# Experts' last sum moved into the matmul accumulator, and the router's last tile taken by halves

## Chip, cores and metric

One core of one Trainium2 chip. The metric is device time of one execution in microseconds (us), the median of several runs. TensorE (PE) multiplies, VectorE (DVE), ScalarE (ACT) and GpSimd (POOL) do the elementwise work, and SyncE (SP) issues the loads from HBM.

## The reference, cut to what matters

256 tokens of width 1024 go through two blocks. In the second layer of the first block a mixer ends in a projection `y @ w_out`, a residual and a layer norm; a router picks two of eight experts for each token; each expert is a gated feed-forward (1024 to 2816 to 1024); the two results are weighed by a softmax over the two logits and summed, and another residual and layer norm follow:

```python
mix = _mixer(u, w_in[layer], ...)                      # ends in  y @ w_out
x = _layernorm(ALPHA * x + (1.0 + g1) * mix, ln1_g, ln1_b)
u = x * (1.0 + sc2) + sh2
top_logits, top_idx = lax.top_k(u @ w_router, 2);  top_w = softmax(top_logits)
ff = sum over the two experts of  top_w * ((silu(u @ Wg) * (u @ Wu)) @ Wd)
x = _layernorm(ALPHA * x + (1.0 + g2) * ff, ln2_g, ln2_b)
```

After that comes a second network, whose first stage is a dense feed-forward on the same `x`.

## The kernel before, in words

Tokens stand in two tiles of 128 (t = 0, 1). Precise products are made of three matmuls (`mm3`, L307): each operand is split into a rounded part "h" and a rest "l", by a ScalarE copy and a VectorE subtraction. For weights these two are L274 and L275, one pair per half unit of 128x1024; they read a raw tile that SP loaded (four raw tiles in turn). Ten half units can be held ahead (`SLOTS`). Every engine works through its own list in the order in which the program wrote it; which half units are converted at which point is written by hand in strings of digits (`TICKS`, one digit per call of `tick`), and `take` forces conversions that have not been made yet.

**The mixer's end** (layer 1). `out_both` L835 projects tile 0 (16 matmuls with 512 columns, L624), takes its residual and statistics (`Norm.stat` L102: L114, L115, bn_stats L123; `fin` L125), and then projects tile 1 with the two halves of the output alternating. After five eighths of tile 1, `Norm1.apply` of tile 0 (L1972) puts its router logits on PE: four transposes L1941, a copy, eight small products L1945, and the same again for the second half; then `settle` L1947. After tile 1 the same follows for tile 1 (`stats` L1957), then `finish` L1981: two scalings L137, the rounding L1987, the residual L1994 and L1995 on VectorE, and only then `settle`. In `moe` (L974) the ranks of both tiles come (L991 to L997, six VectorE operations), the positions (three products L1000 to L1002, a copy L1004), the rest part L1990, the selection matrices `So` (`choose`, four operations L1040), the clearing of the two sums `racc` on GpSimd (L1168), and the gather of the first two experts' tokens (`gather`, 32 matmuls L1070 and L1071), after which the first expert's `gate_up` can start. `load_ahead` (L983) lets SP put later weights into idle tiles, the last two of them into the tiles of the rows G and B that L1994 and L1995 have read.

**The experts' loop** (L1174) runs over 88 chunks, 11 for each expert: `gate_up` of chunk i (24 matmuls), in whose middle the result of chunk i-1 is turned (`turn` L477, hh L315, hl L316), then `down` of chunk i-1 (12 matmuls with 512 columns into two accumulators). Sums of earlier experts are added into `racc` while the next expert runs. In the last expert, chunks 6 and 7 multiply `racc` by the row and add the residual (`residual` L1114). `last` (L1123) then takes the last expert's result: four splits (L315, L316), 16 matmuls with 256 columns through the selection matrix `ST` (L1144, L1145), and per quarter a product with weight and row (L1150), an addition into `racc` (L1152) and bn_stats; after both halves of tile 0 `fin`, the scaling (`scale_all`: L149 and L151, two each) and the turning of x (`to_T`: eight transposes L344, rounding L351, rest L361). Tile 1's norm stands between tile 0's, and its `apply` (scaling and turning) is left in `pend`.

**The feed-forward after it** starts with chunks (tile, chunk) = (0,0), (0,1), (1,0), (1,1); `nxt` in the middle of the first two takes one entry of `pend` each, so that tile 1's `apply` falls into the middle of (0,0).

Of the kernel before, what the change touches and what calls it, by code (L numbers as in the profile page):

```python
# [17 lines left out]
P = 128  # L18
D = 1024
# [47 lines left out]
    "moe_end": "000200000010001",  # L67
# [26 lines left out]
class Norm:  # L94
# [3 lines left out]
    def __init__(self, kern, t, ps, cols, grow=None, mode="T", r=None):  # L98
        self.k, self.t, self.ps, self.cols, self.grow, self.mode = kern, t, ps, cols, grow, mode
        self.r, self.scaled, self.between = r, False, None  # L100
# [18 lines left out]
    def bn(self, hf):  # L119
        k = self.k  # L120
        if hf == 0:
            self.st = k.smp.tile([P, 2, 6], F32, name="st")
        k.nc.vector.bn_stats(out=self.st[:, hf, :], in_=self.r[:, hf * 512:hf * 512 + 512])  # L123
# [16 lines left out]
    def scale_all(self):  # L140
# [7 lines left out]
        for sl in sls:  # L148
            stt(out=r[:, sl], in0=r[:, sl], scalar=self.mv[:, 0:1], in1=k.G[:, sl], op0=ALU.subtract, op1=ALU.mult)  # L149
# [19 lines left out]
class Kern:  # L169
# [317 lines left out]
    def down(self, part, wd, acc, first, last, free, norm=None, mid=None):  # L487

        order = [(i, hf) for hf in range(2) for i in range(2)] if norm else [(i, hf) for i in range(2) for hf in range(2)]
# [126 lines left out]
    def out_proj(self, units, y, acc, kbs, first, last, free, mid=None, ticks=8):  # L616

        for n, kb in enumerate(kbs):
# [17 lines left out]
            if n < ticks:  # L636
                self.tick()

# [11 lines left out]
    def gla_mixer(self, layer, done, start=None, before_out=None):  # L650
# [181 lines left out]
        self.out_both(self.take(4), y, [0, 1, 2, 4, 5, 6, 7, 3], done)  # L832
# [140 lines left out]

    def moe(self, L, gc, bc, grow, done):  # L974

        nc, tc, a, x = self.nc, self.tc, self.a, self.x
        split = self.pend.popleft()
# [8 lines left out]

        gt = self.acp.tile([P, 2, 8, 8], F32, tag="sg", name="gt")
        eq = self.acp.tile([P, 2, 8, 8], F32, tag="sg", name="eq")
        le = L[:, :, :, None].to_broadcast([P, 2, 8, 8])
        lo = L[:, :, None, :].to_broadcast([P, 2, 8, 8])  # L990
        nc.vector.tensor_tensor(out=gt, in0=lo, in1=le, op=ALU.is_gt)  # L991
        nc.vector.tensor_tensor(out=eq, in0=lo, in1=le, op=ALU.is_equal)
        nc.vector.tensor_tensor(out=eq, in0=eq, in1=self.lt[:, None, :, :].to_broadcast([P, 2, 8, 8]), op=ALU.mult)
        nc.vector.tensor_tensor(out=gt, in0=gt, in1=eq, op=ALU.add)
        rank, s1, s2, sel, tmp, W, pos = (sm(n, [P, 2, 8]) for n in ("rank", "s1", "s2", "sel", "tmp", "W", "pos"))
        nc.vector.reduce_sum(out=rank, in_=gt, axis=AX.X)
        nc.vector.tensor_scalar(out=sel, in0=rank, scalar1=2.0, scalar2=None, op0=ALU.is_lt)  # L997
# [3 lines left out]
        nc.tensor.matmul(ps[:, 8:16], self.us, sel[:, 1, :], start=True, stop=False)  # L1001
        nc.tensor.matmul(ps[:, 8:16], self.onesf, sel[:, 0, :], start=False, stop=True)  # L1002
        split()
# [119 lines left out]
        def last(e, acc, norms):  # L1123

            st = ST.pop(e)
            y = []
            for q in range(4):
                if q < 2:
                    yh, yl = (self.acp.tile([P, CW], F32R, tag=g, name="y" + g) for g in ("hh", "hl"))
                else:  # L1130
                    yh, yl = cuts[:, q % 2, 0, :], cuts[:, q % 2, 1, :]
                self.split(yh, yl, acc[q // 2][:, (q % 2) * CW:(q % 2) * CW + CW])
                y.append((yh, yl))
                self.tick(0)
            pss = {}
            for t in range(2):
                ts = slice(t * P, t * P + P)
                for hf in range(2):
                    ps = pss[t, hf] = (self.pgu if t == 0 else self.pacc).tile([P, 512], F32, name="comb",
                                                                               tag="gu" if t == 0 else "acc")  # L1140
                    for q in (0, 1):
                        yh, yl = y[2 * hf + q]
                        pq = ps[:, q * CW:q * CW + CW]
                        nc.tensor.matmul(pq, st[:, ts], yh, start=True, stop=False)  # L1144
                        nc.tensor.matmul(pq, st[:, ts], yl, start=False, stop=True)  # L1145

            def add(t, hf):
                sl = slice(hf * 512, hf * 512 + 512)
                w = mp.tile([P, 512], F32, tag="xs", name="w", bufs=5)
                nc.vector.scalar_tensor_tensor(out=w, in0=pss[t, hf], scalar=W[:, t, e:e + 1], in1=grow()[:, sl],  # L1150
                                               op0=ALU.mult, op1=ALU.mult)
                nc.vector.tensor_tensor(out=racc[t][:, sl], in0=racc[t][:, sl], in1=w, op=ALU.add)  # L1152
                norms[t].bn(hf)
                self.tick(0)
            add(0, 0)
            add(0, 1)
            norms[0].fin()
            self.tick(0)
            norms[0].between = lambda hf: add(1, hf)
            norms[0].apply()  # L1160
            self.tick(0)
            norms[1].fin()
            self.tick(0)
# [5 lines left out]
        for part in range(4):  # L1169
            gather(0, So, part)  # L1170
# [3 lines left out]
        for i in range(n + 1):  # L1174
# [4 lines left out]
            if i < n:  # L1179
# [36 lines left out]
            else:  # L1216
                hT[0] = self.turn(h.pop(i - 1))
            if i:
# [3 lines left out]
                self.down(self.parts_of(hT.pop(0)), self.take(), acc[e], j == 0, j == NCH - 1, True)  # L1222
# [6 lines left out]
        last(NE - 1, acc.pop(NE - 1), norms)  # L1229
        self.close_pool()  # L1230
        self.pend.append(norms[1].apply)
# [629 lines left out]
    def first(self):  # L1861
# [65 lines left out]
        L = self.cp.tile([P, 2, 8], F32, name="L")  # L1927
        mcols = lambda: fold(COL_LN1 + 16, (1, 4), (1, 3))

        class Norm1(Norm):  # L1930
# [16 lines left out]
            def settle(self):  # L1947
                k, t = self.k, self.t
# [7 lines left out]

            def stats(self):  # L1957
                if self.t == 0:
                    return Norm.stats(self)
                for hf in range(2):  # L1960
                    self.stat(hf)
                    self.logits(hf)
                self.fin()
                low, residual = self.finish()
                residual()
                self.settle()
                self.k.pend.append(low)
# [4 lines left out]
            def apply(self):  # L1972
                if self.t == 0:
                    self.logits(0)
                    self.logits(1)
                    self.settle()
                    low, residual = self.finish()
                    residual()
# [211 lines left out]
```

## Time and profile before

| | us |
|---|---|
| median of 3 runs | 2493.15 |
| lowest, highest | 2485.73, 2499.72 |
| the profiled execution's own time | 2487.65 |
| its span (first to last instruction) | 2486.0 |
| PE busy in the span | 2386.9 (96%) |
| DVE, ACT, POOL busy | 1802.7, 1314.6, 44.6 |

The mixer's end lies at about 468 to 507 us of the span, the experts at 507 to 1289, their end and the start of the feed-forward at 1289 to 1328. "Idle before, releaser" in a row says how long the engine had nothing to do before this instruction and what it then waited for.

### The profile page before, as it was taken

To read this page: it belongs to the slowest core of one execution; us is meant where nothing else is said; L and a number is where in the kernel's file an instruction comes from. 1 tells how busy PE (TensorE), PEld (TensorE's weight loads), DVE (VectorE), ACT (ScalarE), POOL (GpSimd) and SP (SyncE) were. 2 spreads that over 40 slices of the span, in tenths; PEclk is the share of its full clock that TensorE was granted. 3 is DMA by queue.
4 is the path that set the end of the run, shared out by engine and by line. 5 is a ranking of instruction groups with operands and counts; after the bars stand their busy time and mean duration, and the time that the engine had idled before them with its cause. 6 is when DMAs were issued, how large, how long until landed. Compare 5 with 4: busy or idle time off the path is not lost. (4 is left out here: it accounts for less than half of the span.)

```text
span 2486.0 us, 34474 instructions
## 1 busy us (share of the span) xinstructions
PE 2386.9 (96%) x13592; PEld 2016.7 (81%) x13592; DVE 1802.7 (73%) x2593; ACT 1314.6 (53%) x1945; POOL 44.6 (2%) x79
## 2 busy tenths in 40 slices
PE   8899989899999999999989999999999998999997
PEld 5769978578788888888867997879987997777996
DVE  6776887689999999999985556555566547556556
ACT  3344444277777777777753444534444444444442
POOL 0000000000000000000000000000000000000000
PEclk9999999899999999999999999999999999999999
DMA  9756957469889999989974544236444644333641
GB/s 361 284 206 241 359 213 277 183 238 371 328 347 372 346 349 364 357 344 358 353 302 169 212 179 167 105 119 246 181 165 160 229 174 149 109 136 124 241 180 62
DMA packets 89208, 600.49 MB, mean 242 GB/s; under 512 B 10288, under 2 KB 11600, under 8 KB 20816
## 3 DMA queue, kind: packets, MB, share of 16 engines
q1 hardware_dynamic: 89040, 598.23, 63.9%
q8 instruction: 108, 1.77, 0.3%
q14 instruction: 60, 0.49, 0.1%
HBM read 597.14 MB, written 1.05 MB: 241 GB/s over the span
## 5 line engine op out<-in xcount | busy, mean ns | idle before, releaser
L275 DVE TENSOR_TENSOR wl<-raw,wh 128x1024 fp32r<-128x1024 f32 (+3 forms) x997 | 1161.4, 1207 | 216.6 <-ACT wh L274 211.0
L274 ACT CAST wh<-raw 128x1024 fp32r<-128x1024 f32 (+3 forms) x997 | 986.6, 1040 | 175.6 <-PE gu L310 99.4
L309 PE MATMUL gu<-uh,wh 128*128 128x256 f32 (+1 forms) x1784 | 504.1, 283 | 0.6 <-ACT cc L785 0.6
L311 PE MATMUL gu<-uh,wl 128*128 128x256 f32 (+1 forms) x1784 | 500.8, 281 | 3.1 <-DVE wl L275 3.1
L310 PE MATMUL gu<-ul,wh 128*128 128x256 f32 (+1 forms) x1784 | 500.3, 280 | 0.0
L309 PEld LDWEIGHTS gu<-uh,wh 128*128 128x128 f32 (+1 forms) x1784 | 334.8, 188 | 6.8 <-issue 1.3
L310 PEld LDWEIGHTS gu<-ul,wh 128*128 128x128 f32 (+1 forms) x1784 | 335.1, 188 | 4.5 <-issue 0.3
L311 PEld LDWEIGHTS gu<-uh,wl 128*128 128x128 f32 (+1 forms) x1784 | 335.5, 188 | 3.8 <-DVE wl L275 3.3
L309 PE MATMUL gu<-wh,xs 128*128 128x512 f32 x704 | 280.8, 399 | 0.1
L311 PE MATMUL gu<-wh,xs 128*128 128x512 f32 x704 | 277.3, 394 | 0.0
L310 PE MATMUL gu<-wl,xs 128*128 128x512 f32 x704 | 276.1, 392 | 0.0
L310 PE MATMUL acc<-wl,hh 128*128 128x512 f32 x432 | 171.2, 396 | 2.6 <-DVE wl L275 2.6
L311 PE MATMUL acc<-wh,hl 128*128 128x512 f32 x432 | 170.5, 395 | 1.6 <-DVE hl L316 1.5
L309 PE MATMUL acc<-wh,hh 128*128 128x512 f32 x432 | 170.9, 396 | 0.5 <-ACT hh L315 0.5
L468 ACT ACTIVATE sg<-gu 128x256 f32<-128x256 f32 x90 | 34.7, 385 | 255.6 <-PE gu L311 255.6
L311 PEld LDWEIGHTS gu<-wh,xs 128*128 128x128 f32 x704 | 132.3, 188 | 29.4
L310 PEld LDWEIGHTS gu<-wl,xs 128*128 128x128 f32 x704 | 132.6, 188 | 26.3
L309 PEld LDWEIGHTS gu<-wh,xs 128*128 128x128 f32 x704 | 132.5, 188 | 26.2 <-issue 0.6
L315 ACT CAST hh<-trh 128x256 fp32r<-128x256 f32 x108 | 40.3, 373 | 198.1 <-PE trh L481 198.1
L311 PE MATMUL acc<-wh,fl 128*128 128x512 f32 x360 | 141.8, 394 | 1.2 <-DVE fl L316 1.2
L309 PE MATMUL acc<-wh,fh 128*128 128x512 f32 x360 | 142.8, 397 | 0.1
L310 PE MATMUL acc<-wl,fh 128*128 128x512 f32 x360 | 141.7, 394 | 0.8 <-DVE wl L275 0.8
(388 smaller groups left out, 3282.4 us busy)
## 6 DMA issues: line engine op xcount, KB each, us to landing
raw<-in_moe_gu_dram SPq DMA_DIRECT2D x175, 1024.0 KB, 5.4
raw<-in_ffn_gu_dram SPq DMA_DIRECT2D x110, 1024.0 KB, 4.9
raw<-in_moe_dn_dram SPq DMA_DIRECT2D x87, 1024.0 KB, 4.9
raw<-in_ffn_dn_dram SPq DMA_DIRECT2D x55, 1024.0 KB, 5.0
raw<-in_ada_w_dram SPq DMA_DIRECT2D x48, 1024.0 KB, 5.2
raw<-in_w_in_dram SPq DMA_DIRECT2D x24, 1024.0 KB, 5.9
raw<-in_fox_in_dram SPq DMA_DIRECT2D x12, 1024.0 KB, 4.9
ww<-in_w_out_dram SPq DMA_DIRECT2D x16, 512.0 KB, 7.4
```

What stands on the lines that cost most here:

```text
L274: nc.scalar.copy(wh[:, :f], r)
L275: nc.vector.tensor_tensor(out=wl[:, :f], in0=r, in1=wh[:, :f].bitcast(F32), op=ALU.subtract)
L309: mm(out, xh, yh, start=first, stop=False)
L310: mm(out, xh, yl, start=False, stop=False)
L311: mm(out, xl, yh, start=False, stop=last)
L315: self.nc.scalar.copy(h, src)
L468: nc.scalar.activation(out=sg, in_=ps[:, :S], func=AF.Silu)
```

## The change

At the mixer's end, tile 1 is projected half by half (`out_halves`), tile 0's logits come after five of the first half's eight matmuls, tile 1's first statistics after the first half and its first logits five matmuls into the second. The ranks are computed per tile in `settle`. The residual of tile 1 is moved behind the gather, as are the clearings of `racc`; the rest part comes before the gather but after `choose`. At the experts' end, `racc` (with the residual) is split into two parts during the last expert and put into the accumulators by products with the identity; the last expert's result is multiplied by weight and row before it goes through `ST`, in halves, behind the first and second half of the last `down`. The norms read the accumulators. Tile 1's scaling is made at once, and its turning moves one chunk later. The digits of `moe_end` put four conversions into the last `gate_up`, and two more are written into the program.

```diff
-    "moe_end": "000200000010001",
+    "moe_end": "220000000000000",
...
     def bn(self, hf):
+        src = self.src[hf] if self.src else self.r[:, hf * 512:hf * 512 + 512]
+        k.nc.vector.bn_stats(out=self.st[:, hf, :], in_=src)
...
     def scale_all(self):
+            stt(out=r[:, sl], in0=self.src[hf] if self.src else r[:, sl], scalar=self.mv[:, 0:1], in1=k.G[:, sl],
+                op0=ALU.subtract, op1=ALU.mult)
...
     def down(...):
+        if norm or then:
+            order = [(i, hf) for hf in range(2) for i in range(2)]
...
+            if then and i == 1:
+                then(hf)
...
+    def out_halves(self, units, y, acc, kbs, mid):
+        for hf in range(2):
+            for n, kb in enumerate(kbs):
...
+                self.nc.tensor.matmul(acc[hf], y(kb), u.halves[half][:, sl], start=n == 0, stop=n == len(kbs) - 1)
+                if hf:
...
+                    if n < 5:
+                        self.tick()
+                if (hf, n) in mid:
+                    mid[hf, n]()
...
     def gla_mixer(...):
-        self.out_both(self.take(4), y, [0, 1, 2, 4, 5, 6, 7, 3], done)
...
+            n0.stats()
+            acc = self.acc2()
+            n1 = done(1, acc)
+            def first_half():
+                n1.stat(0)
+                n0.residual()
+            self.out_halves(uo, y(1), acc, kbs, {(0, 4): n0.apply, (0, 7): first_half,
+                                                 (1, 4): lambda: n1.logits(0)})
+            n1.stat(1)
+            n1.logits(1)
+            n1.fin()
+            n1.settle()
+            n1.scales()
+            self.pend.extend([n1.low, n1.residual])
...
     def moe(...):
+        low, unscaled = self.pend
...
+        nc.tensor.matmul(ps[:, 8:16], self.onesf, sel[:, 0, :], start=True, stop=False)
+        nc.tensor.matmul(ps[:, 8:16], self.us, sel[:, 1, :], start=False, stop=True)
...
+        def base(t):
+            rh = end["h", t] = mp.tile([P, D], F32R, tag="xs", name="rh", bufs=5)
...
+            self.split(rh, rl, racc[t])
+        def slot_weights(e):
+            pc = self.ptr.tile([P, 512], F32, tag="tr", name="cnt")
+            for t in range(2):
+                nc.tensor.matmul(pc[:, 0:1], So[:, t, (e % 2) * P:(e % 2) * P + P].bitcast(F32), W[:, t, e:e + 1],
+                                 start=t == 0, stop=t == 1)
+            ws = end["w"] = sm("ws", [P, 1])
+            nc.vector.tensor_copy(ws, pc[:, 0:1])
...
+        def sums():
+            for t in range(2):
+                for hf in range(2):
...
+                    nc.tensor.matmul(ps, end["i"], end["h", t][:, sl], start=True, stop=False)
+                    nc.tensor.matmul(ps, end["i"], end["l", t][:, sl], start=False, stop=False)
...
+        def share(acc, hf):
...
+            nc.vector.scalar_tensor_tensor(out=f, in0=acc[hf], scalar=end["w"][:, 0:1],
+                                           in1=grow()[:, sl], op0=ALU.mult, op1=ALU.mult)
+            self.split(end["h"][:, sl], end["l"][:, sl], f)
+        def last(e, norms):
+            for hf in range(2):
...
+                for t in range(2):
+                    ts = slice(t * P, t * P + P)
+                    for n in ("h", "l"):
+                        nc.tensor.matmul(end["s", t, hf], st[:, ts], end[n][:, sl], start=False, stop=n == "l")
...
+            norms[0].bn(0)
+            norms[0].bn(1)
+            norms[0].fin()
+            norms[0].scale_all()
+            norms[0].between = norms[1].bn
+            norms[0].apply()
+            self.emit(1)
+            norms[1].fin()
+            norms[1].scale_all()
         So = choose(0)
+        low()
+        for part in range(4):
+            gather(0, So, part)
+        unscaled()
         racc = [...]
...
+                if e == NE - 1 and j == 5:
+                    slot_weights(e)
...
+                if e == NE - 1 and j in (8, 9):
+                    base(j - 8)
...
                 hT[0] = self.turn(h.pop(i - 1))
+                sums()
+                self.emit(1)
...
-        self.pend.append(norms[1].apply)
+        self.pend.extend([None, norms[1].apply])
```

## Rows read from the trace of the kernel before

**Rows 1.** The page, busy time and share of the span by engine

```profile
PE 2386.9 (96%) x13592; PEld 2016.7 (81%) x13592; DVE 1802.7 (73%) x2593; ACT 1314.6 (53%) x1945; POOL 44.6 (2%) x79
```

**Rows 2.** Timeline of the mixer's end: start us, us, engine, instruction

```profile
476.68 0.60 PE L1941 MATMUL pt<-ident,r 128*128 128x128 f32 x4
478.87 0.63 PE L1941 MATMUL pt<-ident,r 128*128 128x128 f32 x4
...
485.45 2.74 PE L624 MATMUL acc<-ww,yf 128*128 128x512 f32 x6
...
492.75 1.88 PE L1945 MATMUL lg<-rwg,ut 128*128 128x8 f32 x8 [0.73 <-ACT ut L1942]
494.28 1.23 DVE L1994 TENSOR_TENSOR x<-r,G 128x1024 f32<-128x1024 f32 x1
...
496.94 0.22 DVE L1952 SCALAR_TENSOR_TENSOR lt<-rsum,nm,lg 128x8 f32<-128x8 f32 x1
...
498.96 0.17 DVE L997 TENSOR_SCALAR sel<-rank 128x16 f32<-128x16 f32 x1
...
500.95 1.11 DVE L1040 TENSOR_SCALAR So<-iota,pos,sel 128x128 fp32r<-128x128 f32 x4
501.86 0.58 PE L1070 MATMUL pg<-So,uh 128*128 128x256 f32 x1 [1.16 <-DVE So L1040]
```

**Rows 3.** Windows: stretch, length, busy of PE, PEld, DVE, ACT, POOL, clock, DMA, GB/s

```profile
477.00:488.20 11.20, 9.83 (x35) 5.03 (x33) 5.75 (x9) 2.22 (x3) 0.00 (x0) 0.85 0.00 0
488.20:501.80 13.60, 5.66 (x30) 4.89 (x30) 11.85 (x26) 2.22 (x3) 2.41 (x3) 0.62 0.47 155
...
547.00:587.00 40.00, 40.00 (x180) 32.56 (x179) 37.23 (x40) 30.08 (x38) 0.00 (x0) 1.00 0.98 377
1304.70:1310.40 5.70, 5.29 (x15) 3.89 (x16) 5.56 (x9) 2.12 (x3) 0.00 (x0) 0.50 0.00 0
...
1501.80:1504.60 2.80, 1.42 (x11) 1.13 (x11) 2.77 (x6) 0.64 (x2) 0.00 (x0) 1.00 0.90 287
```

**Rows 4.** What the load queue (SP) waited for, 488 to 512 us

```profile
SPq L1823 <- DVE x L1994: 6.5, 1, 6.5
```

**Rows 5.** Timeline of the experts' end and the feed-forward's start

```profile
1276.10 0.42 DVE L316 TENSOR_TENSOR hl<-trh,hh 128x256 fp32r<-128x256 f32 x1
...
1278.30 0.39 PE L311 MATMUL acc<-wh,hl 128*128 128x512 f32 x1
...
1290.04 0.50 PE L309 MATMUL acc<-wh,hh 128*128 128x512 f32 x1 [0.46 <-ACT hh L315]
...
1304.76 1.97 PE L344 MATMUL pt<-ident,x 128*128 128x128 f32 x8 [5.56 <-DVE x L151]
...
1306.55 0.79 PE L309 MATMUL gu<-wh,uh 128*128 128x512 f32 x1
...
1314.34 1.94 PE L344 MATMUL pt<-ident,x 128*128 128x128 f32 x8 [2.46 <-DVE x L151]
...
1319.73 0.38 ACT L443 ACTIVATE sg<-gu 128x256 f32<-128x256 f32 x1 [2.83 <-PE gu L311]
...
1328.04 0.40 PE L309 MATMUL acc<-wh,hh 128*128 128x512 f32 x1
```

**Rows 6.** Groups by line and shape, 1286.4 to 1320 us: busy us, mean ns | idle before

```profile
L275 DVE TENSOR_TENSOR wl<-raw,wh 128x1024 fp32r<-128x1024 f32 x5 | 5.9, 1220 | 0.5 <-ACT wh L274 0.5
...
L1150 DVE SCALAR_TENSOR_TENSOR w<-comb,W,grow 128x512 f32<-128x512 f32 x4 | 3.0, 740 | 0.0
L149 DVE SCALAR_TENSOR_TENSOR racc<-racc,mv,G 128x512 f32<-128x512 f32 x4 | 2.8, 746 | 0.0
...
L123 DVE BATCH_NORM_STATS2 st<-racc 128x6 f32<-128x512 f32 x4 | 2.8, 695 | 0.1
L1152 DVE TENSOR_TENSOR racc<-racc,w 128x512 f32<-128x512 f32 x4 | 2.8, 691 | 0.1
...
L351 ACT CAST uh<-pt 128x512 fp32r<-128x512 f32 x4 | 2.3, 586 | 16.2 <-PE pt L344 16.2
```

More of the change, by code (lines that the diff above doesn't have):

```diff
@@ L485, in turn, with down @@
         return hh, hl
-    def down(self, part, wd, acc, first, last, free, norm=None, mid=None):
-        order = [(i, hf) for hf in range(2) for i in range(2)] if norm else [(i, hf) for i in range(2) for hf in range(2)]
+    def down(self, part, wd, acc, first, last, free, norm=None, mid=None, then=None):
+        order = [(i, hf) for i in range(2) for hf in range(2)]
+        if norm or then:
+            order = [(i, hf) for hf in range(2) for i in range(2)]
         for i, hf in order:
@@ L985, in moe @@
                         lambda: self.rowp.tile([P, D], F32, tag="B", name="rawb"))
[L987 to L997, printed above, removed]
+        s1, s2, tmp, W, pos = (sm(n, [P, 2, 8]) for n in ("s1", "s2", "tmp", "W", "pos"))
         ps = self.pgu.tile([P, 512], F32, tag="gu", name="gu")
         nc.tensor.matmul(ps[:, 0:8], self.us, sel[:, 0, :], start=True, stop=True)
-        nc.tensor.matmul(ps[:, 8:16], self.us, sel[:, 1, :], start=True, stop=False)
-        nc.tensor.matmul(ps[:, 8:16], self.onesf, sel[:, 0, :], start=False, stop=True)
-        split()
+        nc.tensor.matmul(ps[:, 8:16], self.onesf, sel[:, 0, :], start=True, stop=False)
+        nc.tensor.matmul(ps[:, 8:16], self.us, sel[:, 1, :], start=False, stop=True)
         nc.vector.tensor_copy(pos.rearrange("p t e -> p (t e)"), ps[:, 0:16])
@@ L1121, in residual @@
                                                op0=ALU.mult, op1=ALU.add)
-        def last(e, acc, norms):
-            st = ST.pop(e)
[L1126 to L1135, printed above, removed]
-            for t in range(2):
[L1137 to L1156, printed above, removed]
@@ L1168, in moe @@
             nc.gpsimd.memset(racc[t], 0.0)
-        for part in range(4):
-            gather(0, So, part)
         n = NE * NCH
@@ L1221, in moe @@
                     acc[e] = self.acc2()
-                self.down(self.parts_of(hT.pop(0)), self.take(), acc[e], j == 0, j == NCH - 1, True)
+                self.down(self.parts_of(hT.pop(0)), self.take(), acc[e], j == 0, j == NCH - 1, True,
+                          then=(lambda hf: share(acc[e], hf)) if i == n else None)
                 if j == NCH - 1 and e < NE - 1:
@@ L1924, in first @@
         self.rate = 1
-        L = self.cp.tile([P, 2, 8], F32, name="L")
+        L, rank, sel = (self.cp.tile([P, 2, 8], F32, name=n) for n in ("L", "rank", "sel"))
         mcols = lambda: fold(COL_LN1 + 16, (1, 4), (1, 3))
@@ L1955, in settle @@
                                                op0=ALU.mult, op1=ALU.add)
[L1957 to L1967, printed above, removed]
+                gt = k.acp.tile([P, 8, 8], F32, tag="sg", name="gt")
+                eq = k.acp.tile([P, 8, 8], F32, tag="sg", name="eq")
+                le = L[:, t, :, None].to_broadcast([P, 8, 8])
+                lo = L[:, t, None, :].to_broadcast([P, 8, 8])
+                tt = nc.vector.tensor_tensor
+                tt(out=gt, in0=lo, in1=le, op=ALU.is_gt)
+                tt(out=eq, in0=lo, in1=le, op=ALU.is_equal)
+                tt(out=eq, in0=eq, in1=k.lt, op=ALU.mult)
+                tt(out=gt, in0=gt, in1=eq, op=ALU.add)
+                nc.vector.reduce_sum(out=rank[:, t], in_=gt, axis=AX.X)
+                nc.vector.tensor_scalar(out=sel[:, t], in0=rank[:, t], scalar1=2.0, scalar2=None, op0=ALU.is_lt)
             def scale_all(self):
```

85 lines of the change are left out of this document (53 added, 32 removed).

## The prediction

> **What bounds the kernel now.** I read the page first: PE is busy 96% of the span [rows 1], so there are some 100 us in all without matmuls, and only what shortens the path between matmuls, or the matmuls themselves, counts. Then the windows: in a stretch of the experts PE works all of its 40 us at full clock and starts an instruction every 40.00/180 = 0.22 us, about 0.23 for a matmul of 512 columns since a few shorter ones are among them; VectorE is busy 93% there and the loads 98% [rows 3]. So the loop is PE's, with little to spare on VectorE and the loads. The gaps lie at the two places that the change touches. Between the end of the mixer's projection and the gather, 13.6 us pass with 5.7 us of PE work at a mean clock of 0.62, where VectorE works 11.9 us [rows 3]: a chain of VectorE steps sets the time. At the experts' end the timeline shows PE idle 5.56 us before tile 0 is turned and 2.46 us before tile 1 is turned in the middle of the first chunk [rows 5], both for VectorE's norm, and the clock is at its lower level, 0.50 (1.2 of 2.4 GHz), as matmuls start again [rows 3].
>
> **Mixer's end.** Tile 1's projection ends at 485.45 + 2.74 = 488.2, the gather starts at 501.86: 13.7 us [rows 2].
> Added ahead of that end: one half of tile 1's logits, now between matmuls. Tile 0's half took 478.87 - 476.68 = 2.2 us [rows 2]. The end moves to 490.4.
> After it, the first half's statistics and logits are gone from the path. What is left: L114 and L115 of one half, 0.69 each by the equally wide L1152 [rows 6], and two handoffs, 1.6 in all; a half of logits, 2.2 at full clock; before, products alone took 1.88 at the lower one [rows 2], so I take 3.0, with 2.2 to 3.6 as ends. Then `settle` and ranks: from L1952 to the end of L997, 499.13 - 496.94 = 2.2 us for two tiles [rows 2]; per tile the five wide ones are half as wide, so 2.0 (1.7 to 2.2). The residual, L1994 and its twin L1995, 2 x 1.23 us [rows 2], no longer stands ahead of `settle`; the rest part no longer stands ahead of the positions. In their place two scalings stand between ranks and the copy of the positions: no row of these two groups has them, they are at most as long as a two-operand step, 0.69 [rows 6]; I take 0.5 each since they have one operand, 1.0 (0.7 to 1.4). PE's last product for the positions runs beside them. The copy 0.2, three of four `So` steps at 1.11/4 [rows 2], 0.85. Sum 1.6 + 3.0 + 2.0 + 1.0 + 0.2 + 0.85 = 8.7, and the gather starts at 499.1, **2.7 us earlier**; the ends of the terms put this at 1.3 to 4.0.
> What covers the moved steps: the rest part (1.22 by the equally long L275 [rows 6]) runs beside the gather's first matmuls, which need its first half only at their fourth; tile 0's residual runs beside the second half of tile 1, 7 us of matmuls. Tile 1's residual, 2.5 us of VectorE, falls into the first expert chunk, ahead of weight conversions. Its cover is the stock of converted half units; if the stock were gone it would cost these 2.5 us. The clearings go to GpSimd, which has 44.6 us of work in the whole span [rows 1]: nothing. On SP's queue the load into G's tile waited 6.5 us for L1994 [rows 4]; it now waits until the residual behind the gather, some 13 us longer, with the load into B's tile and the next ones behind it. Before, those next ones waited for conversions until the first chunk anyway, so 1 MB comes late, at 377 GB/s [rows 3] 2.8 us of loading. Nothing, if the stock lasts; 2.8 us if not.
>
> **Experts' last chunks (added).** `slot_weights`: two products of one column, each in two passes; 0.24 per pass by L1945 (1.88/8 at the lower clock [rows 2]), about 0.5. `base`: two splits, on VectorE 2 x 1.22 [rows 6]. The last chunk but one shows the room: hl is done at 1276.52 and first used at 1278.30 [rows 5], 1.8 us later; with 2.6 us more ahead of it on VectorE, and PE itself 0.5 later, PE waits about 0.4. Sum +0.9 (0.5 to 3.0, the latter if nothing is absorbed).
>
> **Experts' end.** Before the last `down` come eight products with the identity, 8 x 0.23 = 1.85, which fill the wait of 0.46 for hh [rows 5]; so `down` starts at 1290.04 - 0.46 + 0.9 + 1.85 = 1292.3. Its first half is six matmuls, 1.4, and I add 0.3 because hl stands behind two of the four conversions that now sit in this chunk (1.22 each [rows 6]): the first accumulator is whole at 1294.0. Then, for each half, weight and row 0.74 (L1150), rounding 0.59 (L351), rest 0.69 (L1152): 2.02, twice, since VectorE takes them in order, plus six handoffs of some 0.07, gives 1298.5. Two bn_stats, 1.4, and `fin`, 0.45; two L149 and one L151 at 0.75, 2.2, with GpSimd's root beside the L149 pair [rows 6]; the 0.45 is an estimate, two short steps and their handoffs. PE can turn tile 0 at 1302.7 instead of 1304.76: -2.1. The 16 old products and the four additions into `racc` are what this replaces; the new eight products run between the splits. VectorE may lag one or two conversions more (1.2 each): 0 to -3.
> From the turning to the first `gate_up` 1.8 us as before [rows 5]: 1304.5. Chunk (0,0) took from 1306.55 to 1319.7 [rows 5], 13.15 us, of it 2.46 idle and 1.94 turning tile 1. Now it is 24 matmuls without a stop: 5.6 us at full clock, plus half of the stretch at 1.2 GHz; before that stretch lasted until 1310.4 [rows 3], 3.9 us from the first matmul, and I take the same: +1.95. It ends at 1312.0, 7.7 us earlier. Chunk (0,1) took 8.3 us to 1328.04 [rows 5], 2.7 more than its matmuls, since its weights were converted late; one half unit is now ahead, which I put at 1.3 less waiting; added are the turning of tile 1, 1.0 at full clock (half of 1.94), and 0.45 in the next `down`, whose weights then come behind tile 1's rest parts. Net 0.15 worse. **The end gains 7.5 us**, 4 to 10 by the bounds.
>
> **The sum.** -2.7 - 7.5 = -10.2 us. The profiled execution took 2487.65 and would take 2477.4; it lies 5.5 below the median of 2493.15, from which the same sum gives 2483.0. Runs of one kernel spread over 14 us, so about 0.5%, 12.4 us, is what a measurement of this kernel can tell from no change.
>
> **Rivals.**
> *A second fall of the clock.* In the stretch of tile 0's logits and behind it the clock's mean is 0.85 of 11.2 us [rows 3]: 1.7 us of work lost. I count that loss in both kernels alike. The new half stretch of tile 1 could cost it again, or more beside it: 1 to 2 us, total -8.5. Against it: at the end of a later feed-forward 2.8 us with 1.4 us of PE work, a wait and eight transposes, kept 1.00 [rows 3].
> The Trainium skill ("TensorE: Matmul & The Clock Gate", "Part 4: PE-mode transpose") states that transposes do not count as PE work for the clock in the way matmuls do. By that rule the new stretch would count as idle and the second fall would be the likelier case; the row shows a stretch of that kind, of like length, at full clock, and I give this rival 0.1.
> *Supply sets the experts' pace.* With loads at 98% and VectorE at 93% [rows 3] an earlier start of PE might only use up the stock, and the late 1 MB would come on top: the 2.7 us are lost and up to 2.8 are paid, total -7.5 to -4.7, time 2486 to 2488 on the median. Against it: PE shows not one gap in 40 us [rows 3]. 0.15.
> *More than I count.* VectorE's lag before the end is smaller, or the clock rises sooner: the feed-forward's stretch at 1.2 GHz was 3.9 us only after a pause of 5.56 us. Without my terms for lag (0.9 + 0.3) and lower clock (1.95) the total is -13.4, time 2479.8. 0.2.
> *Slower: the lower clock stays.* Between the last `down` and the turning PE has only the eight short products; if matmuls then run at 1.2 GHz not for 3.9 us but on through the next chunks, each us costs half a us. It decides at 10.2/0.5 = 20 us more; if it lasted 50 us more, 2508. For it: the level was 0.50 in this place [rows 3]. Against it: it rose within 6 us of the first transposes there. 0.05.
> *The splits turn out longer than the old additions*, so that the end gains nothing before the turning: -7.5 becomes -5.4, total -8; inside the forecast's own range.
>
> **How the numbers follow.** The forecast, -10.2 with its bounds of -5.5 to -14, has 0.5. Of it some four tenths lie beyond 12.4 us once the spread of a median is added, as does the rival with more: 0.2 + 0.2 = 0.4 faster. The rest of the forecast, the second fall and the supply are within: 0.55. The clock that stays: 0.05. The range takes -19 (bound -14 and 5 of spread) to -2 (supply with spread): 2474 to 2491.
>
> **What would show it.** Right: the gather starts near 499 and the logits' half stands between the projection's matmuls; the turning of tile 0 starts some 13 us after the last `down` begins in place of 14.7, chunk (0,0) has no transposes in it and takes 7 to 8 us, the eight of tile 1 stand in (0,1); hl in the last chunks is waited for under 1 us. Wrong: gaps of PE for wl or for loads in the first five expert chunks, the clock at 0.50 past the first feed-forward chunk, or h and hl of the last chunk more than 2 us late.

## The result and the profile after

The kernel after takes 2462.86 us (median, 2454.25 to 2471.66) against 2490.07 for the kernel before on the same chip: ratio 0.9885, 95% interval 0.9863 to 0.9908, some 28 us. The forecast was 10.2 us, and 2462.86 lies below its range. The profiled execution took 2454.25, its span is 2452.5, 33.5 less than before.

Where these 33.5 us lie is read from ScalarE's first step of each chunk (`sg<-gu`), of which both traces have 198. The difference of their starts, after less before, grows by these steps:

| stretch | us |
|---|---|
| up to the first chunk | -1.6 |
| first dense stage and the start of the next layer | -3.6 |
| the mixer, up to the first expert chunk | -1.8 |
| the experts' 88 chunks | +0.8 |
| **experts' end**, up to chunk (0,0) | -10.5 |
| chunk (0,1) | +0.3 |
| all that follows, four more dense stages among it | -16.8 |

So the experts' end gives 9.4 us, with what was added in the experts and in (0,1). The mixer's end gives nothing in this pair: from the start of its last projection to the first expert matmul the two kernels take the same time (rows at the end of this section), so the 1.8 us of that line lie ahead of the edited place. Over two thirds of the gain lie where the change edits nothing. Below, the timeline of one of the later dense stages: two rows of `sg<-gu`, 13 chunks apart, first of the kernel before, then of the kernel after.

```profile
1939.93 0.39 ACT L468 ACTIVATE sg<-gu 128x256 f32<-128x256 f32 x1 [2.13 <-PE gu L311]
...
2049.27 0.39 ACT L468 ACTIVATE sg<-gu 128x256 f32<-128x256 f32 x1 [1.96 <-PE gu L311]
```

```profile
1913.51 0.39 ACT L470 ACTIVATE sg<-gu 128x256 f32<-128x256 f32 x1 [1.92 <-PE gu L313]
...
2020.28 0.39 ACT L470 ACTIVATE sg<-gu 128x256 f32<-128x256 f32 x1 [1.84 <-PE gu L313]
```

A chunk took 109.34/13 = 8.41 us before and takes 106.77/13 = 8.21 now. There are 90 such chunks (18 in each of five dense stages): 18 us, nearly all of them at the new pace (the first four of the first stage still went at 8.42). PE works without a gap in both, at full clock; it is the matmul itself that is faster. The groups of PE by shape, 1945 to 1995 us, before and after (count, then busy us and mean ns of one):

```profile
L309 PE MATMUL gu<-uh,wh 128*128 128x256 f32 x95 | 26.6, 280 | 0.0
```

```profile
L311 PE MATMUL gu<-uh,wh 128*128 128x256 f32 x99 | 27.4, 277 | 0.0
```

From start to start, the mean over such a stretch is 117.8 ns before and 113.9 after; the matmuls with 512 columns go from 229.8 to 229.0.

The experts' end after, timeline (DVE, PE and ACT rows together):

```profile
1283.25 0.47 PE L1181 MATMUL comb<-rh,identf 128*128 128x512 f32 x1
...
1285.17 0.40 PE L311 MATMUL acc<-wh,hh 128*128 128x512 f32 x1
...
1286.77 0.75 DVE L1190 SCALAR_TENSOR_TENSOR yf<-acc,ws,grow 128x512 f32<-128x512 f32 x1 [0.66 <-PE acc L313]
...
1290.86 1.37 DVE L124 BATCH_NORM_STATS2 st<-comb 128x6 f32<-128x512 f32 x2
...
1294.69 1.84 PE L346 MATMUL pt<-ident,x 128*128 128x128 f32 x8 [2.73 <-DVE x L153]
1296.18 0.78 PE L311 MATMUL gu<-wh,uh 128*128 128x512 f32 x1
...
1303.14 0.39 ACT L445 ACTIVATE sg<-gu 128x256 f32<-128x256 f32 x1 [5.04 <-PE gu L313]
...
1308.41 0.66 PE L346 MATMUL pt<-ident,x 128*128 128x128 f32 x4 [0.54 <-DVE hl L318]
```

From the start of the last `down` to the turning it is now 9.5 us, where before [rows 5] it was 14.7; chunk (0,0) takes 7.0 us from its first matmul, where it took 13.2, and tile 1 is turned in (0,1). The clock there and at the mixer's end, windows of the kernel after (columns as in [rows 3]):

```profile
471.20:480.50 9.30, 9.30 (x17) 4.04 (x18) 7.82 (x17) 2.18 (x3) 0.00 (x0) 0.74 0.00 0
480.50:485.60 5.10, 4.35 (x19) 2.31 (x17) 1.59 (x2) 0.59 (x1) 0.00 (x0) 1.00 0.00 0
485.60:493.60 8.00, 3.00 (x18) 2.63 (x19) 6.14 (x21) 1.72 (x3) 1.46 (x2) 0.75 0.41 131
...
1294.70:1298.50 3.80, 3.76 (x14) 2.97 (x15) 3.46 (x6) 2.12 (x3) 0.00 (x0) 0.56 0.00 0
1298.50:1303.20 4.70, 4.70 (x22) 3.87 (x21) 3.77 (x7) 0.06 (x1) 0.55 (x1) 0.99 0.00 0
```

In this profile the clock is back within 3.8 us of the first turning, where in [rows 3] it still stood at 0.50 in the window that began there and lasted 5.7 us. Over the span the granted clock rose from 0.982 to 0.987.

The mixer's end after, PE's timeline from the start of the projection to the first expert matmul:

```profile
447.30 14.58 PE L630 MATMUL acc<-ww,yf 128*128 128x512 f32 x32
...
471.22 9.46 PE L651 MATMUL acc<-ww,yf 128*128 128x512 f32 x16
480.52 0.60 PE L1999 MATMUL pt<-ident,r 128*128 128x128 f32 x4
...
482.76 2.82 PE L651 MATMUL acc<-ww,yf 128*128 128x512 f32 x6
487.19 0.63 PE L1999 MATMUL pt<-ident,r 128*128 128x128 f32 x4 [1.60 <-DVE r L115]
...
493.61 0.55 PE L1101 MATMUL pg<-So,uh 128*128 128x256 f32 x1 [1.39 <-DVE So L1071]
...
500.34 0.40 PE L311 MATMUL gu<-wh,xs 128*128 128x512 f32 x1
```

The half of tile 1's logits stands between the projection's matmuls (480.52) and the gather follows the projection's end (485.6) by 8.0 us in place of 13.7 [rows 2]. Yet the whole, 447.30 to 500.34, is 53.0 us, and it was 52.9 before, by the same two rows of its trace (the one moved by 7.06 us between the kernels, the other by 6.90):

```profile
454.36 22.48 PE L624 MATMUL acc<-ww,yf 128*128 128x512 f32 x52
...
507.24 0.40 PE L309 MATMUL gu<-wh,xs 128*128 128x512 f32 x1
```

### The profile page after: what moved, and what is told of

The parts are those of the page before. It is cut to its first block, busy times and chain, and to the rows that moved or that the text cites. A ratio compares the mean times of both kernels' runs of the same rounds, so it can differ in the third digit from the quotient of the medians.

```text
span 2452.5 us, 34487 instructions
## 1 busy us (share of the span) xinstructions
PE 2362.6 (96%) x13596; PEld 1995.8 (81%) x13596; DVE 1799.4 (73%) x2596; ACT 1318.0 (54%) x1948; POOL 42.9 (2%) x79
```

## The experiments

**First question: the pace of stages that nobody edited.** What the change does move is memory: `rank` and `sel`, 64 bytes of each partition each, went from the experts' pool to the constants' pool. Every tile that is allocated behind the constants, the converted weights wh and wl among them, lies 128 bytes further on; the activations uh and ul, which lie ahead, stay. Four kernels, on one chip:

```diff
# b1_shift: the kernel before, only this moved
-        rank, s1, s2, sel, tmp, W, pos = (sm(n, [P, 2, 8]) for n in ("rank", "s1", "s2", "sel", "tmp", "W", "pos"))
+        s1, s2, tmp, W, pos = (sm(n, [P, 2, 8]) for n in ("s1", "s2", "tmp", "W", "pos"))
+        rank, sel = self.rank, self.sel
...
-        L = self.cp.tile([P, 2, 8], F32, name="L")
+        L, self.rank, self.sel = (self.cp.tile([P, 2, 8], F32, name=n) for n in ("L", "rank", "sel"))
# a1_noshift: the kernel after, both laid over the router's weights, so that no tile moves
-        L, rank, sel = (self.cp.tile([P, 2, 8], F32, name=n) for n in ("L", "rank", "sel"))
+        L = self.cp.tile([P, 2, 8], F32, name="L")
+        rank, sel = (self.rw[:, o:o + 16].rearrange("p (t e) -> p t e", t=2) for o in (0, 16))
```

The kernel before, unchanged: 

> The kernel before, unchanged. Of the 33.5 us between the two profiled spans, about 11 lie at the two places that the change touches; the rest is a slow drift through stages that the change does not touch: each chunk of the dense feed-forwards takes 8.41 us before and 8.21 after. Theory 'execution': this pace differs from one execution or chip to the next; then this kernel, profiled again, can show chunks of 8.2, and its ratio to the kernel before is 1.000. Theory 'layout': the pace belongs to the program, whose tiles behind the constants lie 128 bytes further on in the change; then this kernel shows 8.41 again in every profile.

The shift alone: 

> The kernel before with the two small tiles rank and sel among the constants, as the change has them, so that all tiles behind lie 128 bytes further on; nothing else differs. 'Layout': dense chunks of 8.2 us, ratio about 0.993 (some 16 us less). 'Execution': the ratio is 1.000 within its interval, and the chunk's length is either.

The kernel after, unchanged: 

> The changed kernel, unchanged. 'Layout': ratio about 0.988 again, dense chunks 8.2 us. 'Execution': the ratio on this chip against the kernel before on the same chip is that of the two places alone, some 11 us of 2490, 0.9955, and the chunk's length is that of the other kernels of this call.

The change without the shift: 

> The changed kernel with rank and sel laid over the router's weights (which are not read any more by then), so that all tiles lie where they lay before. 'Layout': about 0.9955, dense chunks of 8.41 us. 'Execution': the same ratio as the changed kernel itself in this call.

| kernel | median us | ratio (95%) | us a chunk in the five dense stages |
|---|---|---|---|
| b0_again | 2490.16 | 0.9996 (0.9984 to 1.0008) | 8.41 in all |
| b1_shift | 2477.03 | 0.9945 (0.9927 to 0.9964) | 8.42, 8.42, 8.21, 8.21, 8.21 |
| a0_again | 2465.47 | 0.9896 (0.9879 to 0.9914) | 8.21, 8.21, 8.42, 8.21, 8.21 |
| a1_noshift | 2479.33 | 0.9957 (0.9944 to 0.9970) | 8.41 in all |

The shift alone gives 0.55%, 13.7 us; the change without it gives 0.43%, 10.7 us; together about what the kernel after has. a1_noshift also has the old pitch of the matmuls in its dense stages (117.8 ns for 256 columns, 229.8 for 512). In the old layout every stage of every profile goes at 8.41, in the new one the chunks go at one of two paces. Two windows of b1_shift show them (the counts are PE's):

```profile
240.00:290.00 50.00, 50.00 (x358) 46.92 (x357) 42.15 (x63) 24.22 (x33) 0.00 (x0) 1.00 0.85 327
...
1725.00:1775.00 50.00, 50.00 (x369) 47.05 (x368) 26.78 (x31) 22.12 (x30) 0.00 (x0) 1.00 0.53 190
```

Same clock, same busy time, 358 matmuls against 369. What runs beside them doesn't choose the pace: a0_again has the two paces the other way round in the same windows, beside like loads and like work of VectorE.

```profile
240.00:290.00 50.00, 50.00 (x369) 47.06 (x368) 43.10 (x65) 22.96 (x31) 0.00 (x0) 1.00 0.90 348
1725.00:1775.00 50.00, 50.00 (x359) 47.05 (x358) 25.65 (x29) 21.57 (x31) 0.00 (x0) 1.00 0.51 188
```

The table gives the pace of the middle chunks of a stage. Four of the stages kept theirs throughout; in the first it can change. The same group of PE in b1_shift, in its first stage, 203 to 226, 240 to 290 and 316 to 334 us:

```profile
L309 PE MATMUL gu<-uh,wh 128*128 128x256 f32 x52 | 14.4, 277 | 0.0
L309 PE MATMUL gu<-uh,wh 128*128 128x256 f32 x95 | 26.7, 281 | 0.0
L309 PE MATMUL gu<-uh,wh 128*128 128x256 f32 x46 | 12.7, 277 | 0.0
```

The first change lies where PE stood for 0.8 us, the second where 16 transposes stand between the chunks. In the kernel after and in a0_again the first four chunks of this stage are slow and those behind the stop are fast.

**Which tile, and how far.** Unused tiles (`pad`) in the kernel before, ahead of everything, behind the weights, or at the end of the constants:

```diff
# p_front128, ahead of the first tile
+        pad = cp.tile([P, 32], F32, name="pad")
+        nc.gpsimd.memset(pad, 0.0)
# p_row128, in the rows' pool, behind the weights
+        pad = self.rowp.tile([P, 32], F32, name="pad")
...
# p_end64 and p_end256, at the end of the constants
+        pad = self.cp.tile([P, 16], F32, name="pad")     # 64 for p_end256
...
```

> The kernel before with 128 unused bytes ahead of every tile, so that all tiles lie 128 bytes further on and no distance between two tiles changes. Theory A (the distance between the converted weights and the activations that they meet in a matmul decides the pace): all five dense stages keep 8.41 us a chunk, time within 0.2% of the kernel before. Theory B (the place of the weights, or of a tile behind them, decides): 8.21 us in most stages, as in b1_shift, time 8 to 18 us shorter (ratio 0.993 to 0.997). Theory C (the 128 bytes are not the cause; b1_shift was luck of a launch): 8.41, ratio 1.000, but then p_end256 and p_end64 are 8.41 as well.

> The kernel before with 128 unused bytes behind the weights' pool, so that only the rows G and B and the pools of activations behind them (the moving operand of down among them) lie further on, and weights and the activations ahead of them stay. Theory A, that the distance of weights to the moving operand of gate_up_T decides: 8.41 us in all stages, ratio 1.000. Theory B1 (place of the weights): 8.41 as well. Theory B2 (a tile behind the weights, the turned halves or the rows): 8.21 in most stages, ratio 0.993 to 0.997.

> The kernel before with 64 unused bytes at the end of the constants' pool: the same tiles move as in b1_shift, half as far. If only the residue to 128 or more counts (a bank or a line of the memory): its own pace, 8.41 or 8.21 in whole stages. If the old place is a single bad one: 8.21 in most stages, ratio 0.993 to 0.997. If the new place is a single good one: 8.41 in all, ratio 1.000.

> The kernel before with 256 unused bytes at the end of the constants' pool: the same tiles move as in b1_shift, twice as far. If the pace repeats with 256 bytes: 8.41 in all stages, ratio 1.000, as with no shift. If the old place is a single bad one, or the pace repeats with 128 bytes off some other base: 8.21 in most stages, ratio 0.993 to 0.997.

And the kernel after with 32 or 64 bytes more (a_pad32, a_pad64; the same line with 8 or 16 columns, behind `sel`), and with 128 ahead of everything (a_front128):

> The kernel after with the weights and all behind them another 32 bytes further on, so 160 from the old distance. If the pace is set by the distance modulo 256 and falls off smoothly from a best one at 128: 8.3 to 8.45 us a chunk, 2465 to 2480 us. If 128 is an edge between a slow and a fast side, which would explain why stages there run at either pace: 8.21 in all stages, so 2455 to 2460 us in all runs, or 8.45 in all, 2478 or more.

> The same with 64 bytes more, 192 from the old distance. If the distance counts by its size alone to the nearest multiple of 256, this is as p_end64: 8.50 us a chunk in all stages, about 2485 us. If 128 is an edge: as a_pad32, 8.21 or 8.45 and more in all stages.

> The kernel after with 128 unused bytes ahead of every tile: distances as in the kernel after, every tile's own place another. If the distance alone decides: as the kernel after, stages at 8.21 or 8.42, most of them 8.21, 2455 to 2472 us, ratio 0.986 to 0.992. If the place has a part in which of the two paces a stage takes: all five at 8.21 (2455 us) or all at 8.42 (2477 us and more).

| kernel | weights moved against uh, ul | us a chunk | 256 columns, ns | ratio (95%) |
|---|---|---|---|---|
| p_front128 | 0 (all moved by 128) | 8.41 | 117.8 | 0.9999 (0.9986 to 1.0013) |
| p_row128 | 0 (only what lies behind) | 8.45 | 117.8 | 1.0016 (1.0006 to 1.0027) |
| p_end64 | 64 | 8.50 | 119.9 | 1.0023 (1.0007 to 1.0040) |
| a_front128 | 128 (all moved by 128 more) | 8.21 twice, 8.42 thrice | 113.8, 117.8 | 0.9876 (0.9845 to 0.9907) |
| a_pad32 | 160 | 8.44 | 118.7 | 0.9974 (0.9961 to 0.9987) |
| a_pad64 | 192 | 8.52 | 120.0 | 0.9987 (0.9975 to 1.0000) |
| p_end256 | 256 | 8.41 | 117.8 | 1.0004 (0.9991 to 1.0017) |

The ratios are against the kernel before; those of the a_ kernels hold the gain of the edited places too. Moving all tiles together changes nothing (p_front128), so it is the distance between the weights and the activations that counts, not the place (the raw tiles move with the weights, but PE does not read them). 256 bytes bring the old pace back, 64 and 192 are alike and worse than both, and of the seven only 128 is ever fast. At 160 the time, 2484.07 us, lies above the range that I gave for a smooth fall from a best distance: 32 bytes beyond 128 the chunk is already slower than at 0. The same group as above in p_end64, against 280 and 277:

```profile
L309 PE MATMUL gu<-uh,wh 128*128 128x256 f32 x94 | 26.6, 283 | 0.0
```

In p_row128 `gate_up` keeps its pitch and `down`, whose turned halves moved away from the weights, goes from 229.8 to 233.4 ns: its pace hangs on a distance too.

**Which pair.** While a matmul streams uh or ul, weights of the next ones are loaded (PEld is busy 46.9 of the 50.0 us in the first window of b1_shift above). A gap of 128 bytes between uh and ul (p_mid128), and between wh and wl, in the kernel before (p_wl128) and after (a_wl128):

```diff
# p_mid128
+        pad = cp.tile([P, 32], F32, name="pad")
+        nc.gpsimd.memset(pad, 0.0)
         self.ul = cp.tile([P, KB, S], F32R, name="ul")
# p_wl128, a_wl128: once, between the first wh and the first wl
+            if self.gap is None:
+                self.gap = self.wp.tile([P, 32], F32, name="gap")
+                nc.gpsimd.memset(self.gap, 0.0)
             wl = pool_.tile([P, 1024], F32R, tag=k + "l", name="wl", bufs=2 if u.extra else self.SLOTS)
```

> The kernel before with 128 unused bytes between the first part (uh) and the rest part (ul) of the activations, so that ul and the weights move and only uh stays: uh's distance to wh and wl changes, ul's does not. If a matmul is held up by the load of the next weights that runs beside it, each pair on its own: two of three matmuls of gate_up_T gain, 8.28 us a chunk. If the gain needs all pairs at once: 8.41. If only uh counts: 8.21 in most stages.

> The kernel before with 128 unused bytes between the first parts (wh) and the rest parts (wl) of the weights, so that wl and what lies behind the weights move: the load of wl, which runs beside the matmul of wh with ul, is at the new distance, the other loads at the old one. Each pair on its own: one of three matmuls gains, 8.34 us a chunk. All at once or none: 8.41. Whether down's pace changes (its turned halves keep their distance to wl and change it to wh) is read from the pitch of its matmuls, 229.8 ns before and 233.4 in p_row128.

> The kernel after with the same gap between wh and wl: wh stays at the new distance and wl returns to the old one. Each pair on its own: 8.28 us a chunk, as p_mid128, about 2470 us. All at once or none: 8.41, 2478 us. If wl's distance is what makes stages of the kernel after go at either pace: 8.21 or better in all.

p_mid128 went at 8.41 (ratio 0.9996, 0.9983 to 1.0010), p_wl128 at 8.37 (0.9992, 0.9978 to 1.0007), a_wl128 at 8.24 in all five stages (0.9898, 0.9869 to 0.9927), with 113.9 ns for 256 columns and 231.2 for 512. But the 8.37 of p_wl128 is a mean of two: in every stage its chunks take 8.48 and 8.24 us in turn, with 118.9 and 113.9 ns for 256 columns. Two neighbouring chunks of it, with equal numbers of matmuls:

```profile
1946.20:1954.70 8.50, 8.50 (x62) 7.98 (x61) 3.30 (x4) 2.89 (x4) 0.00 (x0) 1.00 0.43 170
1954.70:1962.95 8.25, 8.25 (x62) 7.73 (x61) 5.39 (x6) 4.48 (x7) 0.00 (x0) 1.00 0.75 270
```

So the fast pace does not need a new distance of uh and ul from wh: p_wl128 leaves both at the old one and has it in every second chunk, while p_mid128 puts uh at the new distance from wh and wl and never has it. With wh alone at the new distance (a_wl128) all stages were fast, with wh and wl a stage goes either way. "Each pair on its own" fits none of the three, and no other rule on the pairs was found that fits them all.

Can the fast pace be had for certain, without the loss in `down`? a_wl128 once more, and with another 128 bytes in the rows' pool (a_wl_row128, the line of p_row128):

> The kernel a_wl128 once more, for its spread and its stages: if the gap between wh and wl makes the fast pace certain, all stages are at 8.24 us a chunk again and all runs lie within 14 us, as those of the kernel before do, the median 2458 to 2465 us. If it was luck, stages at 8.42 show up.

> The kernel after with the gap of 128 bytes between wh and wl and another of 128 behind the weights, so that the turned halves that down multiplies regain the distance to wh which they have in the kernel after, and get a new one to wl. If down's pitch is set by the distance to wh: 229.0 ns in place of 231.2 and 8.21 us a chunk in all stages, 2458 us or less, a version that beats the kernel after by some 5 us of its mean. If by the distance to wl: down slower than 231.2 ns, 8.25 or more.

a_wl128b: 2463.24 us, 0.9891 (0.9873 to 0.9908), 8.24 in all stages again, runs from 2461.71 to 2467.24. a_wl_row128: 2455.18 us, 0.9856 (0.9838 to 0.9874), runs from 2451.87 to 2457.43, the lowest median of all. But not for the reason given: its `down` went at 230.7 ns and its chunks at 8.26. Its profile is ahead of a_wl128b's by 9.8 us: 3.8 of them at the mixer's end (below), 4.3 in the experts, whose 87 steps take 773.0 us against 777.3. All its runs are shorter than all of a_wl128b and of the kernel before; its interval overlaps that of the kernel after, so that it beats that one is not shown. Nor is it shown how much of its lead is the layout: the part at the mixer's end goes with the clock, as the next question shows, and a_wl128, the same kernel as a_wl128b, had the mixer's end in the short form too.

**Second question: what each edited place gives.** The change split in the old layout: the mixer's end alone with the old end of the experts (m_only), and the reverse (e_only).

```diff
# m_only, against a1_noshift: parts of the change that are taken back
-    "moe_end": "220000000000000",
+    "moe_end": "000200000010001",
...
-                          then=(lambda hf: share(acc[e], hf)) if i == n else None)
...
-        last(NE - 1, norms)
+        last(NE - 1, acc.pop(NE - 1), norms)
...
# e_only, against a1_noshift: parts of the change that are taken back
-            self.out_halves(uo, y(1), acc, kbs, {(0, 4): n0.apply, (0, 7): first_half,
+        self.out_both(self.take(4), y, [0, 1, 2, 4, 5, 6, 7, 3], done)
...
```

> The mixer's end alone, in the old layout (ranks and choice laid over the router's weights, experts' end as before). The forecast's term: 2.7 us shorter than the kernel before (bounds 1.3 to 4.0), ratio 0.9989. By the traces of before and after the step is 1.8 us: ratio 0.9993. A rival, that the late copies and residual cost the experts their stock of weights: no gain or a loss, ratio 1.000 or more. All dense stages at 8.41 us a chunk.

> The experts' end alone, in the old layout (mixer's end as before). The forecast's term: 7.5 us shorter than the kernel before (bounds 4 to 10), ratio 0.9970. By the traces of before and after the step at the end is 10.5, less 0.8 in the last expert chunks: 9.7 us, ratio 0.9961. Together with m_only it should give what a1_noshift gave, 10.7 us; if the parts help or hinder each other, the sum is off by more than 2 us. All dense stages at 8.41 us a chunk.

e_only: 2481.89 us, ratio 0.9965 (0.9952 to 0.9978), -8.7 us (5.5 to 12). m_only: 2489.50 us, 0.9986 (0.9972 to 1.0001), -3.5 us with an interval that reaches zero (the two medians differ by 0.3 us alone). The sum, 12.2, and a1_noshift's 10.7 agree within their intervals.

One reason for the wide interval may be that the new mixer's end comes in two forms. From the start of the projection to the first expert matmul, ten profiles with the old end took 52.9 to 54.2 us; of ten with the new one five took 49.2 to 49.5 (a0_again, a1_noshift, a_front128, a_wl128, a_wl_row128) and five 52.3 to 53.4 (after, m_only, a_pad32, a_pad64, a_wl128b). PE's timeline of a0_again, to be laid beside that of the kernel after:

```profile
448.33 14.18 PE L630 MATMUL acc<-ww,yf 128*128 128x512 f32 x32
...
471.04 7.11 PE L651 MATMUL acc<-ww,yf 128*128 128x512 f32 x16
477.99 0.60 PE L1999 MATMUL pt<-ident,r 128*128 128x128 f32 x4
...
480.24 2.82 PE L651 MATMUL acc<-ww,yf 128*128 128x512 f32 x6
...
497.79 0.40 PE L311 MATMUL gu<-wh,xs 128*128 128x512 f32 x1
```

```profile
471.00:478.00 7.00, 7.00 (x19) 3.13 (x19) 6.19 (x16) 2.16 (x3) 0.00 (x0) 1.00 0.00 0
```

The 16 matmuls behind tile 0's logits take 7.11 us at a clock of 1.00 (the window above) and 9.46 in the kernel after, at 0.74. The instructions ahead of them are the same. The Trainium skill ("TensorE: Matmul & The Clock Gate", "What's actually happening") says that how many matmuls of one kernel run at the lower clock as it starts varies from run to run; these two profiles of one kernel show the like in its middle, with 2.35 us between them in this row.

The old mixer's end has two forms as well. Behind tile 0's logits it has the last 12 matmuls of the projection, first in the kernel before, then in b0_again, which is the same program:

```profile
481.09 7.09 PE L624 MATMUL acc<-ww,yf 128*128 128x512 f32 x12
```

```profile
485.83 5.40 PE L624 MATMUL acc<-ww,yf 128*128 128x512 f32 x12
```

Five of the ten old profiles have this stretch at 7.09 us, five at 5.40. There it does not set the whole: 52.9 to 53.2 us with the longer stretch, 53.0 to 54.2 with the shorter one, since the clock was low for longer at other places. In the five longer ones of the new form the clock falls already within tile 0's logits, which take 5.2 us in place of 4.4.

## Why the prediction was wrong, and where it was right

**The step that failed** is the sum, "-2.7 - 7.5 = -10.2 us": it has terms for the two edited places only, and so takes for granted that all other stages keep their time. The diff shows `rank` and `sel` in the constants' pool; what that moves was not asked. It has the place of a term of its own, -13.7 us by b1_shift, and some -18 in the profile of after, whose five stages were nearly all fast. Without it the change gives -10.7 (a1_noshift, interval 7.5 to 14), near the forecast of -10.2. That it comes so near is luck in part: in the profile of a1_noshift the mixer's end is 3.7 us shorter, the steps in the experts are 1.8 longer, their end is 10.0 shorter and (0,1) 0.3 longer, so terms that were too small stand beside one that was too small the other way.

**Experts' end**, forecast -7.5 with all that is added: -8.7 by e_only, -9.4 in the profile of after (-10.5, +0.8, +0.3). The -10.5 is no chance of one pair: from the last expert chunk to chunk (0,0), ScalarE's first step of each, ten profiles with the old end take 31.8 to 33.4 us and ten with the new one 22.1 to 23.9. Term by term, forecast and profile: the eight products 1.85 and 1.92; first accumulator whole after 1.7 and 1.6; the two halves through weight, row and rounding 4.5 and 4.1 (1286.77 to 1290.86); statistics, `fin` and scaling 4.2 (the terms given add up to 4.05) and 3.8; to the first `gate_up` 1.8 and 1.5. Chunk (0,0) was to take 7.5 and took 7.0, since the lower clock ended sooner. Nearly every term was a little too long; together these make most of the 1.9. This is the rival "more than I count", in part. The sign "some 13 us" from the last `down` to the turning does not follow from the prediction's own times, which give 1302.7 - 1292.3 = 10.4; measured were 9.5. VectorE did not lag ahead of the turning: no wait for hl before the last `down` is left in the profile; in (0,1) PE still waits 0.76 us for wl and 0.54 for hl. What was added in the experts, +0.9 by the forecast, measured +0.8 in the kernel after, 1.8 in a1_noshift and 3.2 in e_only, above the forecast's upper end of 3.0. In the old layout the 87 steps of the old loop take 773.6 to 774.5 us (before, b0_again, m_only), so there some one to three us were added; with tiles moved the old loop alone reaches 776.3 (p_end64), so the +0.8 of the kernel after says little.

**Mixer's end**, forecast -2.7 (1.3 to 4.0): some -3.5 in the form at full clock (49.5 of a0_again against 52.9), nothing in the other. Its bounds are mis-added: the ends of the terms, as given, make 1.6 to 4.2. Its terms held: half the logits ahead of the end 2.2 (480.52 to 482.76: 2.2), then 8.7 to the gather against 8.0 measured in the kernel after, and 8.4 to 8.8 in the five profiles of the shorter form; the two scalings, for which the prediction had no row, took 1.00 together; tile 1's residual ran in the first chunk without a stop (PE busy 44.7 of the 45 us from 500.3), and the late loads cost nothing, though SP waited 17.3 us for L2055, where it had waited 6.5 [rows 4].

**The second fall of the clock**, 0.1, did not come where I gave it. The new half stretch of tile 1 kept 1.00 (480.5 to 485.6), as the row of the feed-forward in [rows 3] had suggested, and no profile of the new mixer's end has a fall in it. By the rule of the Trainium skill ("TensorE: Matmul & The Clock Gate", "Part 4: PE-mode transpose") the prediction made a fall there the likelier case; none came, but a stretch of 2.2 us between matmuls does not tell whether transposes count.

What cost the mixer's term is the fall at tile 0's logits, the 0.85 of [rows 3], of which the prediction says "I count that loss in both kernels alike". That step failed too: half of the old profiles have no such fall, and in half of the new ones it is longer and takes the whole 3.5 us. Why it comes in some executions and not in others is not settled.

**The other rivals.** Supply did not set the pace: a1_noshift has the whole forecast gain, and PE stood 0.3 us in the first five chunks. The clock did not stay low: 0.99 from 1298.5 on. The end did gain ahead of the turning, 9.5 us in place of 14.7, so the splits did not eat it up.

## What to carry to other kernels

A small tile moved from one pool to another moves every tile behind it. In this kernel, which is bound by matmuls, that alone was worth from -0.55% (b1_shift) to +0.23% (p_end64), so time a change also with the old layout held (lay new tiles over dead ones), before its own steps are credited or blamed. A mean over a stage can hide two paces; look at single chunks before a rule is drawn from it. Where the same matmul's mean duration differs between two profiles at the same granted clock, suspect the layout, and try the few shifts of the weights against the streamed operand on purpose. A sum over the edited places predicts those places; the forecast of the whole needs a line for what the edit changes without being about it.

## What was not expected of the hardware

Matmuls that stream 256 columns of fp32 data started every 113.9, 117.8, 118.7, 119.9 or 120.0 ns, all at full clock and with PE never idle, according to the distance in memory between the streamed operand and the weights: 128, 0 and 256, 160, 64, 192 bytes from the old one. At 128 the matmuls go at 113.9 or at 117.8; the pace holds through whole stages, changed within one only where PE had stopped or transposed between two chunks, and differs between executions of one kernel. With wl alone moved by 128 it changes with every chunk (113.9 and 118.9). The Trainium skill ("TensorE: Matmul & The Clock Gate", "Step-by-step: what each phase is for") says that PE reads the streamed operand and the weights through two independent read ports; by that one would not expect a distance between the two to matter, and here it does. What in the memory or in PE makes it so, and what chooses between the two paces, was not found.
